# Rotary embedding on one core: one GpSimd product per tile, and a strip of one store spread unevenly over the DMA engines

## The chip, the cores and the metric

The kernel runs on one core of one Trainium2 chip. The metric is the device time of one execution in microseconds (us); lower is better. The time given is the median over several executions. One execution was also recorded by the hardware profiler, and every engine time in this document comes from that recording.

## What is computed

The input x has 8 batches of 2048 positions, 8 heads and 64 elements, in float32 (32 MiB). Each head is split into a first and a second half of 32 elements, and the two are rotated by tables that depend on the position alone:

```
x1, x2 = x[..., :32], x[..., 32:]
cos, sin: [2048, 32], the same for every batch and head
out1 = x1 * cos - x2 * sin
out2 = x1 * sin + x2 * cos
out  = concatenate([out1, out2], axis=-1)
```

So the whole input is read once, the whole output is written once, and each element takes two products and one sum.

## The kernel before

**Layout.** A batch is one SBUF tile `xt` of 128 partitions by 8192 floats (32 KB in a partition, 4 MB in all). Partition q holds 16 consecutive positions; one position is `HD` = 512 floats. There are five such buffers (`NBUF`), so the first five batches are loaded at once, and the load of batch 5 waits until batch 0 has been stored, and so on. The batches are counted from 0 in the code and from the first in the text: "the fifth batch" is `b == 4`. The result is written over `xt` in place and stored from there.

**Queues.** Loads are issued by SyncE (SP, line L67; the tables cos and sin at L69 and L70), stores by ScalarE (ACT, L74). Both kinds run on the same 16 DMA engines. Batch 0 is loaded in three and stored in five pieces, the last batch is stored in three pieces, the others in one transfer of 4 MB over 128 partitions. A transfer reports its end through one of eight semaphores, which are handed out in turn; a transfer whose semaphore has been used before waits for that earlier user first.

**Work on a tile.** `rotate` handles mostly a quarter of a batch (`UNIT` = 2048 floats in a partition, four positions); the first and last batch have some halves of that. A tile is of one of three kinds:

- "A", the usual one. GpSimd (POOL) makes x times sin, with the halves swapped and a sign, into `t2` (L121, two products: the second half from the sin table, the first half from the negated table `nsin`). VectorE (DVE) makes x times cos into `t1` in PSUM (L128) and adds `t2`, writing `xt` (L135).
- "B" (the first tile of batches 2, 4 and 5). GpSimd and VectorE make the two products, and TensorE (PE) adds them by multiplying with the unit matrix `eye` into PSUM (L140, L141), in four blocks of 512 floats, with two output buffers `o`. ACT copies each block back to `xt` (L142).
- "C" (the first tile of batches 1 and 3). VectorE makes both products (L128, L145), TensorE adds (L156, L157), ACT copies (L161).

**Buffers.** `t1` of an "A" tile is one PSUM buffer; `t1s` has two SBUF buffers, for "B" and "C" tiles; `t2` has three SBUF buffers. The tables are `cos_sb`, `sin_sb` and `nsin` in SBUF and copies of the first two in PSUM, for VectorE: `sin_ps` made by ACT (L90), `cos_ps` by VectorE (L92). ACT makes `nsin` from `sin_sb` (L89) and `neye` from `eye` (L91).

**Order.** Everything wrapped in `keep` stays in program order on its engine. ACT therefore handles its stores and its copies strictly in the order of the loop: the copies of the sixth batch's first tile come after the store of the fifth batch.

Of the kernel before, what the change touches and what calls it, by code (L numbers as in the profile page):

```python
# [9 lines left out]
@with_exitstack  # L10
def kernel(
    ctx: ExitStack,
    tc: tile.TileContext,
    x: bass.AP,
    cos: bass.AP,
    sin: bass.AP,
    out: bass.AP,
):
    nc = tc.nc
    keep = tc.keep_in_program_order  # L20
    f32 = mybir.dt.float32
    PSUM = bass.MemoryType.PSUM

    B, S, H, D = x.shape
    Dh = D // 2
    P = 128
    HD = H * D
    R = S // P
    ROW = R * HD
    UNIT = 4 * HD  # L30
    NBUF = 5
    C = 512
    last = B - 1

    xv = x.rearrange("b (q r) h d -> b q (r h d)", q=P)
    ov = out.rearrange("b (q r) h d -> b q (r h d)", q=P)
    cos_src = cos.rearrange("(q r) d -> q r d", q=P)
    sin_src = sin.rearrange("(q r) d -> q r d", q=P)

    const_pool = ctx.enter_context(tc.tile_pool(name="const", bufs=1))  # L40
    tab_pool = ctx.enter_context(tc.tile_pool(name="tab", bufs=1, space=PSUM))
    t1_pool = ctx.enter_context(tc.tile_pool(name="t1p", bufs=1, space=PSUM))
    o_pool = ctx.enter_context(tc.tile_pool(name="op", bufs=2, space=PSUM))
    t1s_pool = ctx.enter_context(tc.tile_pool(name="t1s", bufs=2))
    xpool = ctx.enter_context(tc.tile_pool(name="xpool", bufs=NBUF))
    t2_pool = ctx.enter_context(tc.tile_pool(name="t2p", bufs=3))

    cos_sb = const_pool.tile([P, R, Dh], f32, tag="cb")
    sin_sb = const_pool.tile([P, R, Dh], f32, tag="sb")
    nsin = const_pool.tile([P, R, Dh], f32, tag="ns")  # L50
    eye = const_pool.tile([P, P], f32, tag="eye")
    neye = const_pool.tile([P, P], f32, tag="neye")
    cos_ps = tab_pool.tile([P, R, Dh], f32, tag="cp")
    sin_ps = tab_pool.tile([P, R, Dh], f32, tag="sp")

    xts = {}

    def spans(sizes):
        lo = 0
        for n in sizes:  # L60
            yield lo, n
            lo += n

    def load(b):
        xt = xpool.tile([P, ROW], f32, tag="xt", name=f"xt{b}")
        for lo, n in spans([UNIT, UNIT, 2 * UNIT] if b == 0 else [ROW]):
            keep(nc.sync.dma_start(out=xt[:, lo : lo + n], in_=xv[b, :, lo : lo + n]))  # L67
            if b == 0 and lo == 0:
                keep(nc.sync.dma_start(out=cos_sb, in_=cos_src))  # L69
                keep(nc.sync.dma_start(out=sin_sb, in_=sin_src))  # L70
        xts[b] = xt

    def store(b, lo, n):
        keep(nc.scalar.dma_start(out=ov[b, :, lo : lo + n], in_=xts[b][:, lo : lo + n]))  # L74

    for b in range(NBUF):
        load(b)

    nc.gpsimd.memset(eye, 0.0)  # L79
    nc.gpsimd.affine_select(  # L80
        out=eye,
        in_=eye,
        compare_op=mybir.AluOpType.not_equal,
        fill=1.0,
        base=0,
        pattern=[[-1, P]],
        channel_multiplier=1,
    )
    keep(nc.scalar.mul(nsin, sin_sb, -1.0))  # L89
    keep(nc.scalar.copy(sin_ps, sin_sb))  # L90
    keep(nc.scalar.mul(neye, eye, -1.0))  # L91
    keep(nc.vector.tensor_copy(cos_ps, cos_sb))  # L92

    def rep(a, n):
        return dataclasses.replace(a, ap=[a.ap[0][:], a.ap[1][:], [0, n], a.ap[-1][:]])

    kinds = {}
    for b, kind in ((1, "C"), (2, "B"), (3, "C"), (4, "B"), (5, "B")):
        kinds[(b, 0)] = kind

    def rotate(b, lo, n):
        kind = kinds.get((b, lo), "A")
        xt = xts[b][:, lo : lo + n]
        r0 = lo // HD
        nr = n // HD
        xk = xt.rearrange("p (r k d) -> p r k d", r=nr, d=Dh)
        xu = xt.rearrange("p (g u d) -> p g u d", u=2, d=Dh)
        if kind == "A":
            t1 = t1_pool.tile([P, n], f32, tag="t1")
        else:  # L110
            t1 = t1s_pool.tile([P, n], f32, tag="t1s")
        if kind == "C":
            t2 = t1s_pool.tile([P, n], f32, tag="t1s")
        else:
            t2 = t2_pool.tile([P, n], f32, tag="t2")
        t1u = t1.rearrange("p (g u d) -> p g u d", u=2, d=Dh)
        t2u = t2.rearrange("p (g u d) -> p g u d", u=2, d=Dh)
        if kind != "C":
            for u, tab in ((1, sin_sb), (0, nsin)):
                keep(  # L120
                    nc.gpsimd.tensor_mul(  # L121
                        out=t2u[:, :, u, :].rearrange("p (r h) d -> p r h d", h=H),
                        in0=xu[:, :, 1 - u, :].rearrange("p (r h) d -> p r h d", h=H),
                        in1=rep(tab[:, r0 : r0 + nr, :], H),
                    )
                )
        keep(
            nc.vector.tensor_mul(  # L128
                out=t1.rearrange("p (r k d) -> p r k d", r=nr, d=Dh),
                in0=xk,  # L130
                in1=rep(cos_ps[:, r0 : r0 + nr, :], 2 * H),
            )
        )
        if kind == "A":
            keep(nc.vector.tensor_add(out=xt, in0=t1, in1=t2))  # L135
        elif kind == "B":
            for j in range(n // C):
                o = o_pool.tile([P, C], f32, tag="o")
                cs = slice(j * C, (j + 1) * C)
                nc.tensor.matmul(o, eye, t1[:, cs], start=True, stop=False)  # L140
                nc.tensor.matmul(o, eye, t2[:, cs], start=False, stop=True)  # L141
                keep(nc.scalar.copy(xt[:, cs], o))  # L142
        else:
            keep(
                nc.vector.tensor_mul(  # L145
                    out=t2.rearrange("p (r k d) -> p r k d", r=nr, d=Dh),
                    in0=xk,
                    in1=rep(sin_ps[:, r0 : r0 + nr, :], 2 * H),
                )
            )  # L150
            G = C // Dh
            for u in range(2):
                for j in range(n // 2 // C):
                    o = o_pool.tile([P, C], f32, tag="o")
                    gs = slice(j * G, (j + 1) * G)
                    nc.tensor.matmul(o, eye, t1u[:, gs, u, :], start=True, stop=False)  # L156
                    nc.tensor.matmul(  # L157
                        o, eye if u else neye, t2u[:, gs, 1 - u, :], start=False, stop=True
                    )
                    keep(  # L160
                        nc.scalar.copy(  # L161
                            xu[:, gs, u, :], o.rearrange("p (g d) -> p g d", d=Dh)
                        )
                    )

    def pieces(b):
        if b == 0:
            return [2 * HD, 2 * HD, UNIT, UNIT, UNIT]
        if b == last:
            return [UNIT, UNIT, UNIT, 2 * HD, 2 * HD]  # L170
        return [UNIT] * 4

    for b in range(B):
        done = 0
        outs = list(spans([2 * UNIT, UNIT, UNIT] if b == last else [ROW]))
        for lo, n in spans(pieces(b)):
            rotate(b, lo, n)
            done = lo + n
            while outs and sum(outs[0]) <= done:
                whole = outs.pop(0)  # L180
                if b == 0:
                    for part in spans([HD, HD, 2 * HD, UNIT, 2 * UNIT]):
                        store(b, *part)
                else:
                    store(b, *whole)
        if b + NBUF <= last:
            load(b + NBUF)
# [30 lines left out]
```

## Time and profile before

| What | Value |
|---|---|
| Median of 7 runs | 163.76 us (163.53 to 165.64) |
| The profiled execution's own time | 163.6 us |
| Its span on the core | 161.8 us |
| VectorE busy | 140.1 us, 87% |
| GpSimd busy | 138.9 us, 86% |
| TensorE matmul busy | 47.8 us, 30% |
| ScalarE busy | 14.4 us, 9% |
| Moved by DMA | 67.65 MB, 418 GB/s over the span |

The span runs from the first to the last instruction on the core; the rest of the execution's time (1.8 us) lies outside it. The table is to be read with two cautions. A busy share is a mean over the whole span and doesn't say which engine the end waits for. And the DMA engines appear in the profile as queues: q1 carries the loads, q10 the stores, and a queue's share is the time that its packets took, as a share of the time of all 16 engines. A store's line gives the time from its issue to its landing, which includes the time in which its rows stand behind others. Groups of instructions are listed with the mean duration of one in ns, then the idle time of their engine just before them, and what ended it.

### The profile page before, as it was taken

To read this page: it belongs to the slowest core of one execution; us is meant where nothing else is said; L and a number is where in the kernel's file an instruction comes from. 1 tells how busy PE (TensorE), PEld (TensorE's weight loads), DVE (VectorE), ACT (ScalarE), POOL (GpSimd) and SP (SyncE) were. 2 spreads that over 40 slices of the span, in tenths; PEclk is the share of its full clock that TensorE was granted. 3 is DMA by queue.
4 is the path that set the end of the run, shared out by engine and by line. 5 is a ranking of instruction groups with operands and counts; after the bars stand their busy time and mean duration, and the time that the engine had idled before them with its cause. 6 is when DMAs were issued, how large, how long until landed. Compare 5 with 4: busy or idle time off the path is not lost.

```text
span 161.8 us, 470 instructions
## 1 busy us (share of the span) xinstructions
PE 47.8 (30%) x80; PEld 19.0 (12%) x80; DVE 140.1 (87%) x66; ACT 14.4 (9%) x24; POOL 138.9 (86%) x70
## 2 busy tenths in 40 slices
PE   0000000499108940895029902990000000000000
PEld 0000000134003410331014301430000000000000
DVE  0468899999999999999999999999999999999600
ACT  3200000012100220022001310121000000000000
POOL 1299999999999899999994999999999999996000
PEclk9999999999855898579556996597555555555555
DMA  5999999999998989998999999999999999999994
GB/s 184 421 440 493 430 429 413 413 421 437 437 470 350 460 352 458 421 486 389 421 478 397 429 464 397 437 462 407 437 446 413 462 421 413 462 421 413 421 409 207
DMA packets 3746, 67.65 MB, mean 418 GB/s; under 512 B 416, under 2 KB 416, under 8 KB 1056
## 3 DMA queue, kind: packets, MB, share of 16 engines
q1 hardware_dynamic: 1728, 34.08, 49.8%
q10 hardware_dynamic: 2016, 33.56, 48.3%
q14 instruction: 2, 0.02, 0.0%
HBM read 34.08 MB, written 33.55 MB: 418 GB/s over the span
## 4 chain that ended last, share of the span: by engine, by line
DVE 75%; POOL 9%; issue 6%; DMA 3%; SPq 0%; DVEq 0%; POOLq 0%
DVE t L128 40%; DVE xt L135 33%; POOL t L121 9%; DMA sin_sb<-in_sin_dram 3%; DVE t L145 3%; DVEq L135 0%; SPq L69 0%; SPq L67 0%; POOLq L121 0%
## 5 line engine op out<-in xcount | busy, mean ns | idle before, releaser
L121 POOL TENSOR_TENSOR t<-xt,sin_sb 128x1024 f32<-128x1024 f32 (+1 forms) x32 | 71.0, 2220 | 8.8 <-DMA sin_sb<-in_sin_dram 5.8
L128 DVE TENSOR_TENSOR t<-xt,cos_ps 128x2048 f32<-128x2048 f32 (+1 forms) x34 | 73.4, 2167 | 0.8
L121 POOL TENSOR_TENSOR t<-xt,nsin 128x1024 f32<-128x1024 f32 (+1 forms) x32 | 71.1, 2221 | 0.0
L135 DVE TENSOR_TENSOR xt<-t,t 128x2048 f32<-128x2048 f32 (+1 forms) x29 | 62.2, 2145 | 5.4 <-POOL t L121 2.5
L140 PE MATMUL o<-t,eye 128*128 128x512 f32 x24 | 16.6, 782 | 24.0 <-DVE t L128 24.0
L156 PE MATMUL o<-t,eye 128*128 128x512 f32 x16 | 11.9, 848 | 37.6 <-DVE t L128 37.6
L141 PE MATMUL o<-t,eye 128*128 128x512 f32 x24 | 14.9, 709 | 0.0
L142 ACT COPY xt<-o 128x512 f32<-128x512 f32 x12 | 7.0, 586 | 44.8 <-PE o L141 44.8
L140 PEld LDWEIGHTS o<-t,eye 128*128 128x128 f32 x24 | 5.8, 256 | 32.4 <-issue 32.4
L156 PEld LDWEIGHTS o<-t,eye 128*128 128x128 f32 x16 | 3.8, 257 | 42.5 <-POOL t L121 30.6
L161 ACT COPY xt<-o 128x512 f32<-128x512 f32 x8 | 4.7, 586 | 45.3 <-DVE t L128 26.6
L141 PEld LDWEIGHTS o<-t,eye 128*128 128x128 f32 x24 | 5.6, 234 | 8.1 <-issue 8.1
L92 DVE COPY cos_ps<-cos_sb 128x512 f32<-128x512 f32 x1 | 0.7, 695 | 6.3 <-DMA cos_sb<-in_cos_dram 6.3
L157 PE MATMUL o<-t,neye 128*128 128x512 f32 x8 | 5.9, 854 | 0.1
L145 DVE TENSOR_TENSOR t<-xt,sin_ps 128x2048 f32<-128x2048 f32 x2 | 4.6, 2280 | 0.0
L157 PE MATMUL o<-t,eye 128*128 128x512 f32 x8 | 4.1, 592 | 0.0
L157 PEld LDWEIGHTS o<-t,neye 128*128 128x128 f32 x8 | 2.3, 305 | 4.8 <-issue 4.8
L157 PEld LDWEIGHTS o<-t,eye 128*128 128x128 f32 x8 | 1.5, 190 | 1.9 <-issue 1.9
L89 ACT ACT_TABLE_LOAD x1 | 1.3, 1283 | 0.7 <-PEq L202 0.7
L89 ACT ACTIVATE nsin<-sin_sb 128x512 f32<-128x512 f32 x1 | 0.6, 630 | 4.9 <-DMA sin_sb<-in_sin_dram 4.9
L90 ACT COPY sin_ps<-sin_sb 128x512 f32<-128x512 f32 x1 | 0.6, 579 | 0.0
L79 POOL MEMSET eye<- 128x128 f32 x1 | 0.2, 205 | 0.3 <-POOLq L202 0.3
(6 smaller groups left out, 1.0 us busy)
## 6 DMA issues: line engine op xcount, KB each, us to landing
xt<-in_x_dram SPq DMA_DIRECT2D x7, 4096.0 KB, 27.4
out_dram<-xt ACTq DMA_DIRECT2D x6, 4096.0 KB, 33.2
out_dram<-xt ACTq DMA_DIRECT2D x2, 2048.0 KB, 24.2
out_dram<-xt ACTq DMA_DIRECT2D x3, 1024.0 KB, 11.0
xt<-in_x_dram SPq DMA_DIRECT2D x2, 1024.0 KB, 6.1
xt<-in_x_dram SPq DMA_DIRECT2D x1, 2048.0 KB, 11.6
out_dram<-xt ACTq DMA_DIRECT2D x2, 256.0 KB, 18.9
out_dram<-xt ACTq DMA_DIRECT2D x1, 512.0 KB, 32.6
```

Of the source, the lines that this page charges most:

```text
L89: keep(nc.scalar.mul(nsin, sin_sb, -1.0))
L92: keep(nc.vector.tensor_copy(cos_ps, cos_sb))
L121: nc.gpsimd.tensor_mul(out=t2u[:, :, u, :].rearrange("p (r h) d -> p r h d", h=H), in0=xu[:, :, 1 - u, :].rearrange("p (r h) d -> p r h d" ...
L128: nc.vector.tensor_mul(out=t1.rearrange("p (r k d) -> p r k d", r=nr, d=Dh), in0=xk, in1=rep(cos_ps[:, r0 : r0 + nr, :], 2 * H),)
L135: keep(nc.vector.tensor_add(out=xt, in0=t1, in1=t2))
L140: nc.tensor.matmul(o, eye, t1[:, cs], start=True, stop=False)
L141: nc.tensor.matmul(o, eye, t2[:, cs], start=False, stop=True)
L142: keep(nc.scalar.copy(xt[:, cs], o))
L145: nc.vector.tensor_mul(out=t2.rearrange("p (r k d) -> p r k d", r=nr, d=Dh), in0=xk, in1=rep(sin_ps[:, r0 : r0 + nr, :], 2 * H),)
L156: nc.tensor.matmul(o, eye, t1u[:, gs, u, :], start=True, stop=False)
L157: nc.tensor.matmul(o, eye if u else neye, t2u[:, gs, 1 - u, :], start=False, stop=True)
L161: nc.scalar.copy(xu[:, gs, u, :], o.rearrange("p (g d) -> p g d", d=Dh))
```

## The change

GpSimd's two products per tile become one: `swapped` reads x with the two halves of each head exchanged (a step of -32 floats between the halves), and `signed` reads a new table `sgn`, which holds -sin and sin side by side for each position. ACT builds `sgn` with two negations and two copies, for the first four positions and then for the other twelve. The tables `cos_sb` and `sin_sb` move into the two `t1s` buffers. `store` takes a range of partitions, and the fifth batch's store is split: the first 7680 floats of each partition go out over 128 partitions as before, and the last 512 floats (2 KB in a partition, 256 KB in all) go out in six transfers over 80, 14, 12, 10, 8 and 4 partitions.

```diff
-    cos_sb = const_pool.tile([P, R, Dh], f32, tag="cb")
-    sin_sb = const_pool.tile([P, R, Dh], f32, tag="sb")
-    nsin = const_pool.tile([P, R, Dh], f32, tag="ns")
+    cos_sb = t1s_pool.tile([P, R, Dh], f32, tag="t1s", name="cos_sb")
+    sin_sb = t1s_pool.tile([P, R, Dh], f32, tag="t1s", name="sin_sb")
+    sgn = const_pool.tile([P, R, 2, Dh], f32, tag="sg")
...
-    def store(b, lo, n):
-        keep(nc.scalar.dma_start(out=ov[b, :, lo : lo + n], in_=xts[b][:, lo : lo + n]))
+    def store(b, lo, n, ps=slice(0, P)):
+        keep(
+            nc.scalar.dma_start(
+                out=ov[b, ps, lo : lo + n], in_=xts[b][ps, lo : lo + n]
+            )
+        )
...
-    keep(nc.scalar.mul(nsin, sin_sb, -1.0))
+    for lo, hi in ((0, 4), (4, R)):
+        keep(nc.scalar.mul(sgn[:, lo:hi, 0, :], sin_sb[:, lo:hi, :], -1.0))
+        keep(nc.scalar.copy(sgn[:, lo:hi, 1, :], sin_sb[:, lo:hi, :]))
...
+    def swapped(a, nr):
+        return dataclasses.replace(
+            a,
+            offset=a.offset + Dh,
+            ap=[a.ap[0][:], [HD, nr], [D, H], [-Dh, 2], [1, Dh]],
+        )
+
+    def signed(a, nr):
+        return dataclasses.replace(
+            a, ap=[a.ap[0][:], [D, nr], [0, H], [Dh, 2], [1, Dh]]
+        )
...
         if kind != "C":
-            for u, tab in ((1, sin_sb), (0, nsin)):
-                keep(
-                    nc.gpsimd.tensor_mul(
-                        out=t2u[:, :, u, :].rearrange("p (r h) d -> p r h d", h=H),
-                        in0=xu[:, :, 1 - u, :].rearrange("p (r h) d -> p r h d", h=H),
-                        in1=rep(tab[:, r0 : r0 + nr, :], H),
-                    )
+            keep(
+                nc.gpsimd.tensor_mul(
+                    out=t2.rearrange("p (r h u d) -> p r h u d", r=nr, h=H, u=2),
+                    in0=swapped(xt, nr),
+                    in1=signed(sgn[:, r0 : r0 + nr, :, :], nr),
                 )
+            )
...
+                elif b == 4:
+                    store(b, 0, ROW - HD)
+                    p0 = 0
+                    for np_ in (80, 14, 12, 10, 8, 4):
+                        store(b, ROW - HD, HD, slice(p0, p0 + np_))
+                        p0 += np_
```

## The prediction

> **What bounds the kernel now.** I read the shares first, then the transfers, then the tail, and the chain of waits last. The engine shares of the page (VectorE 87%, GpSimd 86%) and the chain that ended last (75% VectorE) suggest a compute bound. The transfer lines of the page contradict them:
>
> ```profile
> DMA  5999999999998989998999999999999999999994
> q1 hardware_dynamic: 1728, 34.08, 49.8%
> q10 hardware_dynamic: 2016, 33.56, 48.3%
> ```
>
> Loads (q1) and stores (q10) together fill 98.1% of the time of 16 DMA engines; only the first and the last slice are not full. The table by stretches shows how it ends:
>
> ```profile
> 141.00:151.00 10.00, 0.00 (x0) 0.00 (x0) 9.69 (x6) 0.00 (x0) 7.38 (x6) 0.50 0.98 421
> 151.00:159.50 8.50, 0.00 (x0) 0.00 (x0) 1.50 (x2) 0.00 (x0) 0.00 (x0) 0.50 0.99 423
> 159.50:160.00 0.50, 0.00 (x0) 0.00 (x0) 0.00 (x0) 0.00 (x0) 0.00 (x0) 0.50 0.40 164
> 160.00:160.50 0.50, 0.00 (x0) 0.00 (x0) 0.00 (x0) 0.00 (x0) 0.00 (x0) 0.50 0.04 16
> 160.50:161.80 1.30, 0.00 (x0) 0.00 (x0) 0.00 (x0) 0.00 (x0) 0.00 (x0) 0.50 0.00 0
> ```
>
> The last two columns are the busy share of the DMA engines and GB/s; VectorE is the third pair. VectorE stops at 152.6 us, and the transfers go on at full rate to 159.5. The compute engines could be some us earlier or later without moving the end. In the last two lines, 0.40 and 0.04 of 16 engines over 0.5 us are 3.2 and 0.32 engine-us. So most engines run dry between 159.5 and 160.0 and one works alone after 160.0, to 160.3 or 160.5. Spread evenly, those 3.5 engine-us would be 0.22 us each: all would end at 159.7. **Perfect balance is worth 0.6 to 0.8 us, and nothing else in this change can shorten the transfers**, whose bytes stay the same.
>
> **What the Trainium skill says.** "DMA: Bandwidth & Descriptors", section "Where 436 GB/s comes from", puts the ceiling of the 16 ports at 435 GB/s; the trace agrees (423 GB/s in the stretch above). The same page, section "Why a DMA increments its semaphore by 16 and not by 1", says that a transfer issued from SP or ACT uses the largest number of engines up to 16 that divides its partitions, the lowest-numbered ones. No transfer of this trace has other than 128 partitions, so nothing here shows it. "GPSIMD Engine Reference", section 3.1, gives 4497 ns for one two-input product of 2048 float32; the trace's pair of half products takes 2354 + 2357 ns, which fits. Its section 7 states half as much time again for reads whose inner step is above 8 bytes; the new operands step by 4 bytes inside a run, so I don't apply it.
>
> **The change, part by part.**
>
> *GpSimd, one product for two (L121).* The groups by shape:
>
> ```profile
> L121 POOL TENSOR_TENSOR t<-xt,nsin 128x1024 f32<-128x1024 f32 x28 | 66.0, 2357 | 0.0
> L121 POOL TENSOR_TENSOR t<-xt,sin_sb 128x1024 f32<-128x1024 f32 x28 | 65.9, 2354 | 3.1 <-DVE xt L135 2.6
> L121 POOL TENSOR_TENSOR t<-xt,sin_sb 128x512 f32<-128x512 f32 x4 | 5.1, 1277 | 5.8 <-DMA sin_sb<-in_sin_dram 5.8
> ```
>
> From 512 to 1024 elements the mean grows by 1.08 us, so the fixed part is 1.277 - 1.08 = 0.2 us and a 2048 product is 2.36 + 2 x 1.08 = 4.52 us, against 4.71 for the pair. Thirty-two pairs save 0.19 each: 6 us of GpSimd's busy time, 5 us by the starts (halves follow each other every 2.28 us, less than they last). Wins on the path: none. GpSimd now waits for VectorE (2.6 us in all) more than the reverse, VectorE's own 140.1 us hardly shrink, and the end hangs on the transfers. I take 0. Were that cover gone, VectorE's 2.5 us of waits for GpSimd (page, L135) would be the most it brings.
>
> *The signed table (L89).* Today GpSimd's first product waits for the sin load only and starts at 7.06 us. Now it waits for ACT's negation and copy of the first four rows. ACT's rows are 0.630 us for 512 elements and 0.300 for 128 (neye), a copy of 512 is 0.579; so 0.30 + 0.25 from 6.94 gives a start at about 7.55, 0.5 later. The product of the first tile ends near 9.9 instead of 9.54, and the first store leaves ACT near 11.2 instead of 10.8. Four passes instead of one delay sin_ps by 0.9 us to about 9; VectorE needs it at 30.5. The cos and sin tables now occupy the two t1s buffers, wanted back at 28.3 (first "C" tile) and free by 9. All hidden: from 8 to 12 us the DMA engines are full with loads.
>
> *The strip, on the DMA engines.* By the rule cited, 80 partitions give every engine 5 rows of 2 KB, and 14, 12, 10, 8, 4 give one row to engines 0-13, 0-11, 0-9, 0-7, 0-3. Engines 0-3 get 10 rows, 4-7 get 9, 8-9 get 8, 10-11 get 7, 12-13 get 6, 14-15 get 5, where each had 8. Prices from the DMA view of short windows, share x 16 engines x window / packets: a 32 KB row 1.213 us (126 to 127 us: 91.0%, 12 packets), a 2 KB row 0.084 us (13 to 22: 5.6% of 144 engine-us, 96 packets), a completion packet 0.009. Cutting eight rows to 30 KB saves 8 x 0.076 = 0.61 us per engine. Engines 14-15: -0.61 + 5 x 0.084 + 0.01 = -0.18; 12-13: -0.08; 10-11: +0.01; 8-9: +0.10; 4-7: +0.20; 0-3: +0.29. The mean is +0.10 us: the strip costs engine time. It wins at most 0.18 us, if the last engine is 14 or 15, and loses 0.29 if it is 0 to 3. The trace does not number engines.
>
> *The strip, on ACT's queue.* The six added issues cost 6 x 0.34 = 2.0 us of an engine that is busy 9%. Their waits matter more. The order of the two built programs shows eight DMA semaphores handed out in turn, and a transfer first waits for the previous user of its semaphore. After the main part (issued at 97.8) the strips of 80 and 14 go at once, 12 waits for the sixth batch's load (landed 87.8), 10 for the third store (99.2), 8 for the seventh load (107.3), and **the last, 4 partitions, for the fourth store, landed 81.5 + 37.0 = 118.5**. The later stores get other predecessors too: the sixth batch's store now waits for the eighth load, 99.3 + 27.4 = 126.7, instead of leaving at 114.2.
>
> Queued behind the strip on ACT are the four copies of the sixth batch's first tile (103.8 to 109.5 now), held until 118.9 and then done by about 123, as TensorE, with two output buffers, makes its third and fourth block only after them. TensorE thereby holds that tile's t2 buffer till about 122; by the waits of the built program GpSimd asks for it back only at the eighth batch's first tile, near 129, and the two other t2 buffers keep it ahead of VectorE meanwhile. No load waits for the fifth or a later store, so SP is untouched. The sixth store, issued at 126.7 + 0.34, has its first packet about 1 us later (the first load: issued 0.74, DMA busy from 1.7): 128.1. The fifth store's engines are busy till 131.9, less about 1 us of spread and 0.4 of receipt: the first runs dry near 130.4. **Margin 2.3 us; cost 0.** Seventh and eighth batch stores wait for parts of the fifth, landed by 132, and leave at 133 or later anyway.
>
> *Instruction fetch.* The queue of instructions moves one 8 KB packet in 94-95 and one in 111-112 us, 0.30 us each on one engine. GpSimd has 32 instructions fewer, so one may go; ACT has 9 more rows, so one may come. Between -0.3 and +0.3 on one engine; I take 0.
>
> Sum: the last engine moves by -0.5 to +0.6 at the outside, likely -0.2 to +0.2. On the profiled execution's 163.6 (span 161.8 plus 1.8 outside) that is 163.4 to 163.8; the median of the runs is 0.16 above that execution. I take 163.6, 0.16 under the median of 163.76.
>
> **The rivals.**
>
> *Balance pays in full.* The even share ends all engines together: at most the 0.6 to 0.8 us above, 163.0 to 163.2, a little lower with a fetch gone. For it: one engine is alone at the end. Against: 0.18 is the largest relief of any engine, and what made the last one late need not follow its number.
>
> *GpSimd's product is slower, and the result slower.* Place: L121; the swapped operand walks three levels, one backward, which no row shows. GpSimd ends at 148.4; VectorE takes its last product at 151.4 (3.0 spare), and the last store, issued at 152.6, is needed about 2.5 us (1 MB) plus 1 of latency before 160.5, so at 157.0 (4.4 spare). GpSimd may thus lose 7.4 us on 137.4, 30 full tiles: it decides from 4.83 us per product, 10% above the 4.40 between starts. At 15% (5.06) it costs 30 x 0.48 - 7.4 = 7 us: 171. Below, unrolled runs could also gain, which is hidden. Against: pairs with runs of 32 cost just what the skill gives for one whole product, so the walk seems free.
>
> *The ACT wait opens a hole.* If the eighth load lands or the sixth store starts more than 2.3 us later than reckoned, all engines idle for the rest: 4 us late gives +1.7, 165.5.
>
> *The shares don't follow the numbers.* Other engines than named take the strip; the tail moves by up to 0.3 either way, 163.5 to 164.1.
>
> **How the numbers follow.** Main forecast 0.62, 163.3 to 164.0; balance in full 0.16, of which half goes below 162.94; slower GpSimd 0.09; hole on ACT 0.05; other shares 0.08, mostly within. Half a per cent, 0.82 us, is about what a measurement of this kernel can tell from no change. A few hundredths go to slower for a fetch and the low engines adding up: faster 0.10, same 0.73, slower 0.17. The range runs from 163.0 to 164.5 and leaves out most of the two slow mechanisms and the best end of the balance.
>
> **What would show it.** Right: L121's successor at 4.4 to 4.6 us x28, GpSimd near 133 us busy; ACT's copies of the sixth batch at 119 to 123 instead of 104 to 110; the sixth store's issue at 127; DMA share 0.98 or more to 159.5; the end within 0.3 of 160.5. Wrong: a DMA share under 0.9 anywhere between 126 and 133 (hole), GpSimd over 4.8 us a product, or a tail after 159.5 that vanishes (balance in full).

## The result, and the profile after

The changed kernel takes **165.62 us** (median of 23 runs, 163.66 to 196.99) beside 163.7 us before (60 runs): a ratio of **1.0074, 95% interval 1.0052 to 1.0095**, slower by 0.5 to 1.0%. Forecast were 163.6 us and no measurable change. The ratio leaves disturbed executions out and is not the quotient of the two medians. The profiled execution took 164.55 us, with a span of 162.6; that is under the median, so its trace shows less of the loss than most executions have.

The lines of the page that answer to those of before, busy share in 40 slices and queues (packets, MB, share of 16 engines):

```profile
DMA  5999999999999999999999999999999899999993
q1 hardware_dynamic: 1728, 34.08, 49.5%
q10 hardware_dynamic: 2208, 33.56, 48.3%
```

Same bytes, and 192 packets more for stores: 128 rows of the strip and 64 completions (16 + 14 + 12 + 10 + 8 + 4), which agrees with the numbers of engines that the prediction took for the six transfers. The share of both queues together fell from 98.1% to 97.8%. The groups of GpSimd's product by shape (busy us, mean ns, then idle time before it):

```profile
L138 POOL TENSOR_TENSOR t<-xt,sgn 128x2048 f32<-128x2048 f32 x28 | 125.8, 4525 | 5.1 <-DVE xt L152 5.1
...
L138 POOL TENSOR_TENSOR t<-xt,sgn 128x1024 f32<-128x1024 f32 x4 | 9.3, 2356 | 6.1 <-ACT sgn L95 6.1
```

A whole product takes 4525 ns; GpSimd's busy time fell from 138.9 to 135.8 us, and VectorE's stayed at 140.1. The second line shows the one new wait: the first product now waits for ACT's table (L95). The table by stretches (pairs for PE, PEld, VectorE, ACT, GpSimd, then TensorE's clock; last two columns DMA share and GB/s) of the changed kernel:

```profile
118.00:126.00 8.00, 5.42 (x8) 2.08 (x8) 7.83 (x4) 2.25 (x4) 8.00 (x3) 0.72 1.02 440
126.00:134.00 8.00, 0.00 (x0) 0.00 (x0) 7.72 (x5) 0.00 (x0) 8.00 (x2) 0.71 0.97 413
151.00:159.50 8.50, 0.00 (x0) 0.00 (x0) 1.86 (x2) 0.00 (x0) 0.00 (x0) 0.50 0.99 419
159.50:160.00 0.50, 0.00 (x0) 0.00 (x0) 0.00 (x0) 0.00 (x0) 0.00 (x0) 0.50 0.71 295
160.00:160.50 0.50, 0.00 (x0) 0.00 (x0) 0.00 (x0) 0.00 (x0) 0.00 (x0) 0.50 0.16 66
160.50:161.50 1.00, 0.00 (x0) 0.00 (x0) 0.00 (x0) 0.00 (x0) 0.00 (x0) 0.50 0.10 41
```

Around the strip, from 118 to 134 us, the DMA engines stay full. What is new is at the end. At 159.5 to 160.0 the share is 0.71 where it was 0.40, and 0.16 and 0.10 follow. This view counts a packet whole in the stretch where it starts, so the shares say how much work was begun late, and not how many engines were busy. The single packets of the trace say that: each engine closes its last transfer with a packet of 4 bytes, and 13 of these end by 160.22 us, the last three at 160.75, 161.17 and 161.46. Before, the last one ended at 160.53. In the product without the strip (the experiment "product only" below) the tail is longer still:

```profile
160.50:161.50 1.00, 0.00 (x0) 0.00 (x0) 0.00 (x0) 0.00 (x0) 0.00 (x0) 0.50 0.21 90
161.50:162.60 1.10, 0.00 (x0) 0.00 (x0) 0.00 (x0) 0.00 (x0) 0.00 (x0) 0.50 0.16 67
162.60:164.30 1.70, 0.00 (x0) 0.00 (x0) 0.00 (x0) 0.00 (x0) 0.00 (x0) 0.50 0.02 10
```

Here 13 engines are done by 160.56 us and three end at 162.51, 162.99 and 163.02, some 3 us after most others. So the question is not what makes the transfers slower, but what makes **three engines** late.

### The profile page after: what moved, and what is told of

Same layout as the page of the kernel before. It is cut to its first block, busy times and chain, and to the rows that moved or that the text cites. A ratio compares the mean times of both kernels' runs of the same rounds, so it can differ in the third digit from the quotient of the medians.

```text
span 162.6 us, 449 instructions
## 1 busy us (share of the span) xinstructions
PE 51.1 (31%) x80; PEld 20.1 (12%) x80; DVE 140.1 (86%) x66; ACT 15.0 (9%) x27; POOL 135.8 (83%) x38
## 4 chain that ended last, share of the span: by engine, by line
DVE 74%; POOL 8%; issue 8%; DMA 3%; SPq 0%; DVEq 0%; ACT 0%
DVE t L145 40%; DVE xt L152 31%; POOL t L138 8%; DMA sin_sb<-in_sin_dram 3%; DVE t L162 3%; DVEq L152 0%; SPq L69 0%; SPq L67 0%; ACT sgn L95 0%; ACT sgn L94 0%
## 5 line engine op out<-in xcount | busy, mean ns | idle before, releaser
L138 POOL TENSOR_TENSOR t<-xt,sgn 128x2048 f32<-128x2048 f32 (+1 forms) x32 | 135.1, 4254 | 11.3 <-ACT sgn L95 6.1
L157 PE MATMUL o<-t,eye 128*128 128x512 f32 x24 | 18.4, 863 | 35.9 <-DVE t L145 23.5
L173 PE MATMUL o<-t,eye 128*128 128x512 f32 x16 | 11.8, 843 | 37.2 <-DVE t L145 37.2
L158 PE MATMUL o<-t,eye 128*128 128x512 f32 x24 | 15.7, 745 | 0.0
L157 PEld LDWEIGHTS o<-t,eye 128*128 128x128 f32 x24 | 6.1, 273 | 45.2 <-issue 31.9
L173 PEld LDWEIGHTS o<-t,eye 128*128 128x128 f32 x16 | 3.9, 257 | 42.5 <-POOL t L138 30.6
L158 PEld LDWEIGHTS o<-t,eye 128*128 128x128 f32 x24 | 6.1, 256 | 9.2 <-issue 9.2
L174 PE MATMUL o<-t,neye 128*128 128x512 f32 x8 | 6.6, 940 | 0.2 <-DVE t L162 0.2
L174 PE MATMUL o<-t,eye 128*128 128x512 f32 x8 | 4.1, 592 | 0.0
L174 PEld LDWEIGHTS o<-t,eye 128*128 128x128 f32 x8 | 1.5, 190 | 1.9 <-issue 1.9
L94 ACT ACTIVATE sgn<-sin_sb 128x128 f32<-128x128 f32 (+1 forms) x2 | 0.8, 413 | 4.8 <-DMA sin_sb<-in_sin_dram 4.8
L95 ACT COPY sgn<-sin_sb 128x128 f32<-128x128 f32 (+1 forms) x2 | 0.8, 388 | 0.0
```

What stands on the lines that cost most here:

```text
L94: keep(nc.scalar.mul(sgn[:, lo:hi, 0, :], sin_sb[:, lo:hi, :], -1.0))
L95: keep(nc.scalar.copy(sgn[:, lo:hi, 1, :], sin_sb[:, lo:hi, :]))
L138: nc.gpsimd.tensor_mul(out=t2.rearrange("p (r h u d) -> p r h u d", r=nr, h=H, u=2), in0=swapped(xt, nr), in1=signed(sgn[:, r0 : r0 + nr, ...
L174: nc.tensor.matmul(o, eye if u else neye, t2u[:, gs, 1 - u, :], start=False, stop=True)
```

## The experiments

Each was timed in five rounds beside the kernel before. The expectations name their theories by letters. At the start they were that the strip costs more than reckoned (A), or that the single product does, by disturbing the transfers (B). Once the strip had fallen, a third was added (C): the signed table delays the first store, and this changes the order in which some DMA engines take their rows.

### Which part of the change: four runs

Product alone, with the fifth batch's store whole:

```diff
-                elif b == 4:
-                    store(b, 0, ROW - HD)
...
-                        store(b, ROW - HD, HD, slice(p0, p0 + np_))
-                        p0 += np_
```

> The changed kernel with the fifth batch stored whole again, so only the single GpSimd product and the table sgn are left of the change. Theory A (the strip costs the time: its waits on ACT's queue or its small transfers): the time is that of the kernel before, 163.4 to 163.9 us, with little scatter, and ACT's copies of the sixth batch stand at 104 to 110 us. Theory B (the single product costs it, by disturbing transfers out of SBUF although GpSimd itself is no slower): the time scatters from 163.7 to 166 us, with a median near 165.5, as in the changed kernel.

Strip alone, on the kernel before: `store` gets its range of partitions, and the branch for `b == 4` is added; GpSimd keeps its two products.

```diff
+                elif b == 4:
+                    store(b, 0, ROW - HD)
+                    p0 = 0
+                    for np_ in (80, 14, 12, 10, 8, 4):
+                        store(b, ROW - HD, HD, slice(p0, p0 + np_))
+                        p0 += np_
```

> The kernel before with the strip alone: GpSimd makes two products as before, the fifth batch's store is split as in the change. Theory A: 165 to 166 us in the median, scattered from 163.7 to 166. Theory B: 163.3 to 163.8 us, no scatter, the DMA engines ending closer together than before.

The changed kernel with the strip in one transfer, even over the engines:

```diff
-                    for np_ in (80, 14, 12, 10, 8, 4):
+                    for np_ in (128,):
```

> The changed kernel with the strip as one transfer over 128 partitions, so every DMA engine gets 8 of its rows, and ACT is not held: its one wait is for a store that landed long before. Theory A1 (the waits of the strip on ACT's queue and of the later stores cost the time): 163.4 to 163.9 us. Theory A2 (the rows of 2 KB cost it, wherever they go): above 164.5 us. Theory A3 (the uneven shares or the transfers over few partitions cost it): 163.4 to 163.9 us, as A1; a run with the same shares and no waits has to tell these two apart. Theory B: scatter up to 166 us.

And the changed kernel unaltered, once more beside these three:

> The changed kernel again, unchanged, beside the others on one chip. All theories: scatter from 163.7 to 166.2 us, median 165 to 166; its recording is wanted for where the late DMA engine loses its time: theory A1 sees all engines idle for some tenths between 126 and 134 us, theory A3 one or a few engines lasting to the end alone, theory B store packets that last longer than 1.21 us a row of 32 KB while the tiles are worked on.

| Kernel | Median, us | Ratio to before, 95% |
|---|---|---|
| product only | 165.41 | 1.0098 (1.0069 to 1.0127) |
| strip only | 163.96 | 0.9993 (0.9962 to 1.0024) |
| even strip | 165.89 | 1.0118 (1.0073 to 1.0162) |
| changed, again | 165.3 | 1.0093 (1.0068 to 1.0117) |

The loss belongs to the product, and it is there in full without the strip. The strip alone brings nothing and costs nothing that can be measured. So the shares over 80, 14, 12, 10, 8 and 4 partitions are not the cause.

Yet the product's engine, GpSimd, was faster, and VectorE as busy as before. The start is where the product lengthens something. The changed kernel's timeline (start, duration, idle time before it and what ended it):

```profile
7.44 9.11 POOL L138 TENSOR_TENSOR t<-xt,sgn 128x1024 f32<-128x1024 f32 x3 [6.14 <-ACT sgn L95]
...
9.81 1.22 DVE L152 TENSOR_TENSOR xt<-t,t 128x1024 f32<-128x1024 f32 x1 [1.67 <-POOL t L138]
...
11.07 0.86 ACTq L75 DMA_DIRECT2D out_dram<-xt  x2
```

and the same three of the kernel before:

```profile
7.06 1.26 POOL L121 TENSOR_TENSOR t<-xt,sin_sb 128x512 f32<-128x512 f32 x1 [5.76 <-DMA sin_sb<-in_sin_dram]
...
9.57 1.23 DVE L135 TENSOR_TENSOR xt<-t,t 128x1024 f32<-128x1024 f32 x1 [1.34 <-POOL t L121]
...
10.82 0.86 ACTq L74 DMA_DIRECT2D out_dram<-xt  x2
```

The first store leaves ACT 0.25 us later (0.33 and 0.34 in product only and even strip). Two windows of the DMA view tell what that does. First, 14.3 to 15.4 us: the second batch's load (q1) is under way and the first store's 2 KB rows (q10) come in. Before (queue: packets, MB, share):

```profile
q1 hardware_dynamic: 16, 0.52, 110.3%
q10 hardware_dynamic: 16, 0.03, 7.6%
```

Changed, then even strip:

```profile
q10 hardware_dynamic: 13, 0.03, 6.2%
```

```profile
q10 hardware_dynamic: 10, 0.02, 4.8%
```

Before, all 16 engines take one row of the store between the first and the second 32 KB row of that load. Changed, only 13 do, and in even strip only 10: the store came just too late for the others, which take their second load row first. "DMA: Bandwidth & Descriptors", section "Queues, rings and completion order", of the Trainium skill says that an engine goes round between its queues packet by packet; the trace agrees, 16 load and 16 store packets in one window. An engine that missed this turn has then moved one load row more than the others, and its store rows come later.

Second, 65 to 71 us, where stores are under way and the sixth batch's load, issued at 63.6, comes in. Before:

```profile
DMA packets 80, 2.62 MB, mean 437 GB/s; under 512 B 0, under 2 KB 0, under 8 KB 0
...
q10 hardware_dynamic: 49, 1.61, 61.9%
q1 hardware_dynamic: 31, 1.02, 39.3%
```

Even strip:

```profile
DMA packets 68, 2.23 MB, mean 371 GB/s; under 512 B 0, under 2 KB 0, under 8 KB 0
...
q10 hardware_dynamic: 42, 1.38, 66.4%
q1 hardware_dynamic: 26, 0.85, 32.9%
```

The engines are as full (101% and 99%) and move 15% less. The mean store row takes 0.664 x 96 engine-us / 42 = 1.52 us where it took 0.619 x 96 / 49 = 1.21. The single packets between 64.5 and 71 us show that this mean is of two kinds:

| Kernel | Engines that missed the turn at 14 us | Store rows of over 2 us | GB/s, 65 to 71 us |
|---|---|---|---|
| before | 0 | 0 of 49 | 437 |
| changed | 3 | 3 of 52 | 415 |
| changed, again | 3 | 5 of 52 | 393 |
| product only | 3 | 6 of 52 | 404 |
| even strip | 6 | 12 of 48 | 371 |

The other rows are at 1.2 to 1.5 us. In product only and even strip there are just two slow rows for each engine that missed its turn, in the changed kernel one. A slow row takes 2.05 to 2.43 us; two cost their engine 2.1 to 2.4 us, most of what the three late engines of product only are behind. The profile gives packets no engine number. But an engine can be followed from packet to packet: nearly every packet starts 3 or 4 ns before the one ahead of it on the same engine ends, and every engine has the same rows in the same order up to the strip. Followed so, the six engines of even strip that missed the turn at 14 us are the six with two slow store rows each, and the six that end last, at 162.21 to 162.91 us; all others end by 160.46. In product only the three engines with slow rows are the three that end last; two of them had missed the turn, and for the third the times fit two engines.

### Is it the first store's time? Four runs

If so, the loss must go when the first product starts as early as before, with the new product everywhere else. Changed, in the first tile only:

```diff
+            if b == 0 and lo == 0:
+                for u, tab in ((1, sin_sb), (0, sgn[:, :, 0, :])):
+                    keep(
+                        nc.gpsimd.tensor_mul(
+                            out=t2u[:, :, u, :].rearrange("p (r h) d -> p r h d", h=H),
+                            in0=xu[:, :, 1 - u, :].rearrange("p (r h) d -> p r h d", h=H),
+                            in1=rep(tab[:, r0 : r0 + nr, :], H),
+                        )
+                    )
+            else:
...
```

> The changed kernel, strip included, but GpSimd makes the very first tile's product in two halves again, the second half from the sin table alone, so that it need not wait for ACT's copy and the first store can leave ACT at about 10.8 us as before, not at 11.1; the other 31 products stay single. Theory C (the 0.3 us by which the first store leaves later puts some DMA engines one load row out of step, and these lose 2 us in the fifth load's neighbourhood near 66 us): 163.3 to 163.9 us, all store rows of 66 to 70 us at 1.21 us. Theory B (the single product itself disturbs the transfers): 165 to 166 us, as the changed kernel.

And it must come when the kernel before is delayed. There, in the first tile only, the half that needs `nsin` goes first:

```diff
-            for u, tab in ((1, sin_sb), (0, nsin)):
+            order = ((1, sin_sb), (0, nsin))
+            if b == 0 and lo == 0:
+                order = order[::-1]
+            for u, tab in order:
```

> The kernel before with one edit: in the first tile alone GpSimd makes the half with the negated table first, so it has to wait for ACT's negation (0.6 us) and the first store leaves ACT near 11.3 instead of 10.8 us. No single product, no table sgn, no strip. Theory C: 164.5 to 166.5 us, scattered, with store rows of more than 2 us near 66 to 70 us on some DMA engines. Theory B: 163.5 to 163.9 us, unchanged.

The same delay without a change to GpSimd's work, by repeated copies on ACT ahead of its first store, five or eight of them:

```diff
     keep(nc.scalar.mul(neye, eye, -1.0))
+    for _ in range(5):
+        keep(nc.scalar.copy(sin_ps, sin_sb))
```

> The kernel before with ACT copying sin to its PSUM table five times more before its first store, so that GpSimd and VectorE run exactly as before and only the issue of the first stores slips by 0.4 to 0.8 us. Theory C: 164.5 to 166.5 us. Theory B, and any theory in which a late product of GpSimd or a late sum of VectorE is what matters: 163.5 to 163.9 us.

> As the run with five copies, with eight: the first stores leave near 13 us, about 2 us later than before. Theory C in the form that the mixture costs (some engines in step, some not): all engines miss the first turn, all are one load row ahead alike, and the time comes back under 164.5. Theory C in the form that being ahead costs each engine: every engine loses about 2 us near 66, 165.5 to 166.5 with little scatter. Theory B: 163.5 to 163.9 us.

| Kernel | First store leaves ACT | Engines that took the turn | GB/s 65 to 71 | GB/s 76 to 81 | Median, us | Ratio, 95% |
|---|---|---|---|---|---|---|
| first tile in halves | 10.86 | 16 | 431 | 459 | 164.06 | 1.0026 (1.0013 to 1.0038) |
| before, negated half first | 11.38 | 3 | 415 | 347 | 164.53 | 1.0047 (1.0032 to 1.0062) |
| before, 5 copies | 10.69 | 16 | 431 | 446 | 163.74 | 1.0006 (0.9987 to 1.0026) |
| before, 8 copies | 12.53 | 0 | 431 | 341 | 164.18 | 1.0016 (0.9998 to 1.0034) |

One tile out of 32 in two halves takes away most of the loss: from 1.0074 and 1.0093 to 1.0026. The reverse in the kernel before brings a loss. The five copies gave no delay at all: the store left at 10.69, without waiting for the copies to run out, so this run says only that the copies by themselves cost nothing. For the eight copies there were two forms of theory C on record: each late engine loses about 2 us (165.5 to 166.5 us), or only a mixture of engines in and out of step costs, and the time comes back under 164.5. The time, 164.18 us, rules out the first. It doesn't prove the second, for the engines are not all alike here. No engine takes the turn at 14 us; the next window, 15.4 to 16.7 us, shows

```profile
q10 hardware_dynamic: 10, 0.02, 4.0%
```

So ten take their first store row after two rows of the load, and six only after three. The stretch of 65 to 71 us runs at 431 GB/s, and what is slow is another one. Before, by stretches:

```profile
65.00:71.00 6.00, 5.67 (x7) 2.39 (x8) 5.90 (x4) 0.18 (x1) 6.00 (x4) 0.53 1.01 437
76.00:81.00 5.00, 0.00 (x0) 0.00 (x0) 4.86 (x3) 0.00 (x0) 5.00 (x3) 0.65 1.06 452
```

Eight copies:

```profile
65.00:71.00 6.00, 5.70 (x7) 2.53 (x8) 5.90 (x4) 0.20 (x1) 6.00 (x4) 0.50 1.00 431
76.00:81.00 5.00, 0.00 (x0) 0.00 (x0) 4.86 (x3) 0.00 (x0) 5.00 (x3) 0.70 0.96 341
```

VectorE (third pair) and GpSimd (fifth) do the same in both; only the transfers differ. The rate of this stretch alone is no measure of a loss, as the strip-only kernel has 387 GB/s there and loses nothing that can be measured. A longer delay did not bring a greater loss: 0.16% (with zero inside its interval) against 0.7 to 1.2%.

### ACT alone, in between: two runs

Five copies left the first store where it was, and eight delayed it by 1.7 us. Two runs aim in between: five copies and a second negation of `eye`, and six copies.

```diff
+    for _ in range(5):
+        keep(nc.scalar.copy(sin_ps, sin_sb))
+    keep(nc.scalar.mul(neye, eye, -1.0))
```

> The kernel before with five further copies of sin and one further small negation on ACT before its first store. GpSimd and VectorE run as before; the first store should leave ACT at 10.9 to 11.2 us, as in the changed kernel (with five copies alone it left at 10.7, as early as before, so that run delayed nothing). Theory C (a first store that reaches the DMA engines while the sixth of their load rows is under way splits them into two groups out of step, and a minority loses about 2 us near 66 us): 164.3 to 166 us if it leaves at 11.0 or later, with store rows of about 2.4 us between 65 and 71 us. Any theory of GpSimd or of the tables: 163.5 to 163.9 us.

```diff
+    for _ in range(6):
+        keep(nc.scalar.copy(sin_ps, sin_sb))
```

> As the run before, with six copies: the first store leaves ACT at about 11.3 us, GpSimd and VectorE untouched. Theory C: most DMA engines miss the turn, a few do not; 164.3 to 165.5 us, like the run that made the negated half first (164.5 at 11.38 us). Any theory of GpSimd or of the tables: 163.5 to 163.9 us.

The first again delayed nothing: the store left at 10.83 (10.9 to 11.2 expected), and the time is 163.67 us, 0.9993 (0.9975 to 1.001). The second hit. Its timeline and its window of 14.3 to 15.4 us:

```profile
8.20 3.68 ACT L93 COPY sin_ps<-sin_sb 128x512 f32<-128x512 f32 x6
11.36 0.86 ACTq L74 DMA_DIRECT2D out_dram<-xt  x2
```

```profile
q10 hardware_dynamic: 7, 0.01, 3.3%
```

Seven of 16 engines took the turn; 164.46 us, **1.0049 (1.0027 to 1.0071)**. GpSimd's and VectorE's instructions are those of before, and only the store's issue is 0.54 us later. The ratio is that of the negated half first, whose store left at the same time. This shows that the first store's lateness is enough by itself to bring a loss. But here 65 to 71 us has no store row above 1.6 us, and 76 to 81 us has 347 GB/s: with nine engines out of step the loss comes where the eight copies had theirs. Following the engines as above shows who bears it:

| Kernel | Smaller group at the first store | Its slow rows, us | It ends at, us | Others end by, us |
|---|---|---|---|---|
| changed | 3 that missed the turn | one store row each, 2.05 to 2.40 | 160.75 to 161.46 | 160.22 |
| product only | 3 that missed | two store rows each, 2.16 to 2.43 | 162.51 to 163.02 | 160.56 |
| even strip | 6 that missed | two store rows each, 2.07 to 2.43 | 162.21 to 162.91 | 160.46 |
| before, negated half first | 3 that took it | a load row near 77 us each, 2.13 to 2.73 | 161.07 to 161.40 | 160.74 |
| before, 6 copies | 7 that took it | a load row near 77 us in five, 2.05 to 2.30 | five at 160.66 to 161.51 | 160.69 |
| before, 8 copies | 6 that waited for a third load row | a load row at 77 to 79 us, 2.07 to 2.26 | 160.57 to 161.12 | 160.49 |

Where the times of two engines coincide, the assignment stays open (two engines of the changed kernel, one each of product only, six copies and eight copies). As far as the engines can be followed, it is each time the *smaller* group that has the slowest rows and ends last, whether it is the late one or the early one. So what costs is that the engines disagree, more than that the store is late. A first store that is late for all 16 engines alike was not run.

### What remains, and the best form of the change: two runs

The halves in the first tile, this time without the strip (both edits above together):

> The changed kernel with the first tile's product in two halves and the fifth batch stored whole: the single product without the late first store and without the strip. Theory C: 163.4 to 163.9 us. If the 0.3% that the run with halves and strip lost against the kernel before belongs to the strip, it is gone here; if to the single product, this run too stands at 164.0 to 164.3.

164.05 us, 1.002 (1.0004 to 1.0036), beside 1.0026 with the strip. What remains above before is not the strip's.

The changed kernel with the loads of the two tables exchanged, all 32 products single and the strip in place:

```diff
+                keep(nc.sync.dma_start(out=sin_sb, in_=sin_src))
                 keep(nc.sync.dma_start(out=cos_sb, in_=cos_src))
-                keep(nc.sync.dma_start(out=sin_sb, in_=sin_src))
```

> The changed kernel, all 32 products single and the strip in place, with the order of two loads exchanged: sin before cos, so that ACT starts on the signed table 0.6 us earlier and the first store leaves near 10.5 us. Theory C: 163.4 to 164.1 us, no store row of over 1.5 us between 65 and 71 us. Theory B (the single product disturbs the transfers): 165 to 166 us.

Its timeline, and the stretch:

```profile
6.77 9.12 POOL L138 TENSOR_TENSOR t<-xt,sgn 128x1024 f32<-128x1024 f32 x3 [5.47 <-ACT sgn L95]
...
10.41 0.86 ACTq L75 DMA_DIRECT2D out_dram<-xt  x2
```

```profile
65.00:71.00 6.00, 6.00 (x10) 2.37 (x10) 5.90 (x3) 1.17 (x2) 6.00 (x2) 0.71 0.99 426
```

Sin arrives earlier, ACT starts the table earlier, and the store leaves at 10.41. All 16 engines take the turn, no store row is above 1.3 us, and the stretch has the 426 GB/s of strip only. **163.9 us (21 runs, 163.7 to 164.53), 1.0009 (0.9989 to 1.0028)**: the change as it was forecast, with no effect that can be measured. Among the forms with the single product it has the lowest ratio, though the intervals of the two with halves overlap its own; no kernel here is shown faster than before.

## Why the prediction was wrong

The step that failed is **"The signed table (L89)"**, in its last sentence: "All hidden: from 8 to 12 us the DMA engines are full with loads". Its sizes were nearly right: product at 7.44 (said 7.55), first store at 11.07 to 11.16 (said 11.2). Also right was that the engines are full then. The conclusion was not: full engines mean that a late store leaves no gap, and not that it makes no difference which row comes next. With 0.25 us more, 3 of 16 engines take another row first, and 50 us later store rows of these engines take up to twice their time; two such rows cost an engine up to 2.4 us. The term costed at 0 is worth 0.7 to 1.2% in the four runs that have it in full, 1.2 to 1.9 us.

With it falls "nothing else in this change can shorten the transfers, whose bytes stay the same". The time of the transfers also hangs on the order of rows, which the sum took as given: the same 32 KB row takes 1.21 or 2.43 us. The sum therefore had no such term, and none of the rivals was this one. The rivals on the slow side were GpSimd's product, a hole in the middle of the kernel and other shares of the strip; none looked at the start.

The other steps, point by point:

- *GpSimd's product* of 2048: 4525 ns, predicted 4.52 us. The price of "GPSIMD Engine Reference", section 3.1, 4497 ns, is one that the page gives for an add; this product with its backward walk takes as long within 1%. The rival of a slower product falls. The saving was overestimated: busy time fell by 3.1 us and not by 6, since whole products start 4.47 to 4.49 us apart where they follow each other freely (predicted 4.40), and pairs of halves took 4.56. It is hidden, as said: VectorE's busy time is unchanged.
- *The strip on ACT's queue.* The chain of semaphores, as predicted; the timeline of the changed kernel:

```profile
98.22 20.08 ACTq L75 DMA_DIRECT2D out_dram<-xt  x7
118.42 1.07 ACT L159 COPY xt<-o 128x512 f32<-128x512 f32 x2 [24.60 <-DMA out_dram<-xt]
...
124.51 0.59 ACT L159 COPY xt<-o 128x512 f32<-128x512 f32 x1 [1.13 <-PE o L158]
...
127.52 25.82 ACTq L75 DMA_DIRECT2D out_dram<-xt  x5
```

  The seven issues of the fifth store take 20 us, the copies follow from 118.4 to 125.1 (predicted 118.9 to 123), and the sixth store leaves at 127.5 (predicted 126.7). The margin of 2.3 us held: shares of 1.02 and 0.97 from 118 to 134 us, no hole.
- *The strip on the DMA engines.* It did not level the engines. In strip only, where the first store leaves as early as before, their last packets end between 159.77 and 161.04 us; before, between 159.53 and 160.53. In time it brought nothing measurable: strip only is 0.9993 (0.9962 to 1.0024). The predicted best gain of 0.18 us is a tenth of a per cent, within that interval. The rival "balance pays in full" (163.0 to 163.2, a gain of 0.3 to 0.5%) has only its lower end in that interval.
- *Instruction fetch*: still two packets, but the one of 111 us is gone and one comes at 147.6. The prediction had 0.30 us for a fetch, and that was too little: before, the load row that follows the fetch of 94.2 us takes 1.75 us instead of 1.21, so that its engine loses 0.31 + 0.53 = 0.84 us. Followed by its packets, this is the engine that ends last, at 160.53 us. So the tail that the strip was to shorten hung on a fetch, as far as this trace shows, and not on the number of an engine. No run isolates what a fetch is worth in the kernel's time.

**Open.** Why store rows of a few late engines run at half speed near 66 us, and why it is load rows near 77 us when most are late, was not tried; that the same byte count is slower in another order is shown, the reason is not. The runs with the first store early again take most or all of the loss away, but no run without the single product loses more than 0.5%, and none makes just three to six engines miss the turn. Each kernel has one trace, so whether the scatter of the changed kernel (164.11 to 166.53 us when it was run again) comes from more or fewer engines missing the turn is not shown. Nor is it known what the 0.1 to 0.3% are that the two kernels with halves in the first tile keep.

## What to carry to other kernels

When the DMA engines bound a kernel, "the engines are full at that time" is no reason to cost a delay at nothing. Here the first transfer of the second queue decided in which order each engine took its rows, and three engines out of step were enough to move the end. So an edit near the start is to be checked for what it does to the first store's time, and the count of packets per queue in that short window shows whether all engines do the same. A cheap test is to shift that one transfer alone, both ways; the cheapest mend here was to load first the table that is now needed first.

## What the runs showed of the hardware

- A quarter of a microsecond at 11 us decides over 1.2 to 1.9 us at the end. The point lies between 10.86 us (all engines take the turn) and 11.06 us (three do not); at 11.36 to 11.38 nine to thirteen do not, at 12.53 none does, and then ten take the next turn and six the one after.
- The loss doesn't grow with the delay: 1.0074 to 1.0118 with 3 to 6 engines missing the turn, 1.0047 to 1.0049 with 9 to 13, 1.0016 (0.9998 to 1.0034) with all 16 missing it, of which 6 wait one load row longer than the rest.
- The smaller group of engines, late or early, has the slowest rows: 32 KB rows of 2.05 to 2.73 us, where the usual row takes 1.21.
- An instruction fetch of 8 KB costs its engine more than its own 0.31 us: the 32 KB load row after it took 1.75 us (fetch at 94 us) and 1.43 (at 111), both before the change, instead of 1.21.
- A store's issue on ACT does not wait until the copies ahead of it have ended: with six it left at 11.36, and the copies ran to 8.20 + 3.68 = 11.88. With five it left at 10.69 and 10.83 (10.82 before).
